# Multiplying the last quarter of each expert's down weights as plain float32 instead of splitting it

## The chip, the cores and the metric

The kernel runs on one core of one Trainium2 chip. The metric is the device time of one execution in microseconds (us). A core has five engines that run side by side, each through its own list of instructions in order: TensorE (PE, with its weight loads shown as PEld), VectorE (DVE), ScalarE (ACT), GpSimd (POOL) and SyncE (SP), which here starts most DMA transfers. They wait for each other through semaphores.

## The reference

One layer of a decoder for 2048 tokens of width 1024: a mixer (projection, matrix memory, a recurrence, output projection), a router, and a mixture of 32 experts. Each token goes to two experts. Only the experts matter for the change:

```
gates = gates / jnp.sum(gates, axis=-1, keepdims=True)
...
def expert_block(args):
    xb, e = args
    hid = jax.nn.silu(xb @ w_gate[e]) * (xb @ w_up[e])
    return hid @ w_down[e]
```

Tokens are sorted by expert and cut into blocks of up to 128. `w_gate[e]` and `w_up[e]` are 1024 x 512, `w_down[e]` is 512 x 1024, all float32. The result of a block is scaled by the gates and added to each token's row; a layer norm ends the layer.

## The kernel before

The products are made to float32 accuracy from pieces: a float32 operand w is split into a rounded part `wh` in the type float32r, which TensorE multiplies in one pass, and the remainder `wl = w - wh`, and a product x·w is the three products xh·wh + xl·wh + xh·wl. For weights, ACT makes `wh` (`copy`, L1313) and DVE makes `wl` (`sub`, L1316).

The experts are the last phase, `moe_phase`. The 32 experts are taken in a fixed order. Each has 12 raw tiles of 128 x 1024 (512 KB each): four of gate, four of up, four of down (a "quarter" of down is 128 rows of the 512). `load` starts their transfers on SP's queue into 9 buffers with the tag raw (`RAW = 39 - 2 * SPL`, SPL = 15). `high` makes the `wh` of a tile, `low` its `wl` and then starts the load of the tile nine further on, since the subtraction was the last reader of the raw tile. `wh` and `wl` have 15 buffers each, so all 12 of an expert and the first three of the next (`AHEAD = 3`) are split at a time. Raw tiles, `wh` and `wl` together fill 39 tiles.

`block` computes up to 128 tokens: 24 matmuls of 512 columns for gate, Silu on ACT, 48 matmuls of 256 columns for up in two halves, the products with Silu(gate) on DVE (L1445, tile th), four transposes of the hidden values through PE, the split of these into `hh` (ACT) and `hl` (DVE), then `down(k)` for the four quarters, six matmuls each:

```
for a, b in ((hh, dh), (hh, dl), (hl, dh)):
    for n in range(2):
        mm(pd[n], a[:, ks], b[:, n * CH:(n + 1) * CH], ...
```

The order on each engine is the order in which the code is written (`keep`). In the first block of an expert the splits stand between PE's steps: tiles 3 to 8 ahead of the gate's matmuls, `high` of 9 to 11 behind Silu, `low` of the down tiles between the steps of up and down, the last of them (`low(e, 11)`) together with the transposed rows of the next expert (`xh`, `xl`), and at the end the three tiles of the next expert. Then ACT scales the two halves of the result into yo (L1515), POOL multiplies yo by a row (`scaled`, L1597) and starts the scattered addition to memory (L1601), both behind the branch on the expert's token count (L1718).

An expert with more than 128 tokens takes that branch: a rest of at most 64 tokens goes to `narrow` (under the branch L1684), which packs the rounded part and the remainder of 64 tokens side by side in 128 columns, so that four matmuls make a quarter of down instead of six; a larger rest takes `block` again. Only the first block of an expert loads and splits.

Of the kernel before, what the change touches and what calls it, by code (L numbers as in the profile page):

```python
# [7 lines left out]
F32 = mybir.dt.float32  # L8
F32R = mybir.dt.float32r
# [6 lines left out]
P = 128  # L16
D = 1024
# [3 lines left out]
CH = 512  # L21
# [5 lines left out]
NE = 32  # L27
DFF = 512
# [1260 lines left out]
def moe_phase(tc, A, cn, u2_dram, lists, z_dram, mods_dram, out, nstat=4):  # L1289
    nc = tc.nc  # L1290
    ident, cnt = cn["ident"], cn["cnt"]
    SPL, LATE = 15, 9
    RAW, AHEAD = 39 - 2 * SPL, SPL - 12
    NZ = 6

    order = [4 * (i % 8) + i // 8 for i in range(NE)]
# [1 line left out]
    with ExitStack() as es:  # L1298
# [7 lines left out]
        def mm(*a, **k):  # L1306
            keep(nc.tensor.matmul(*a, **k))  # L1307
# [4 lines left out]
        def copy(o, i, scale=1.0):  # L1312
            keep(nc.scalar.activation(o, i, AF.Copy, scale=scale))  # L1313

        def sub(o, a, b):
            keep(nc.vector.tensor_sub(o, a, b))  # L1316


        raws = {}
        ws = {}  # L1320
        nload = [0]

        def load(upto, queue=nc.sync):
            while nload[0] < min(upto, 12 * NE):
                e, i = divmod(nload[0], 12)
                e = order[e]
                t = wp.tile([P, D], F32, tag="raw", name="raw", bufs=RAW)
                if i < 8:
                    k = i % 4
                    src = A["w_up" if i >= 4 else "w_gate"][0, e, 256 * k:256 * (k + 1), :]  # L1330
                    op = queue.dma_start(t.rearrange("p (k f) -> p k f", f=DFF), src.rearrange("(k p) f -> p k f", p=P))
                else:
                    op = queue.dma_start(t, A["w_down"][0, e, P * (i - 8):P * (i - 7), :])
                if queue is nc.gpsimd:
                    keep(op)
                raws[nload[0]] = t
                nload[0] += 1

        def high(e, *ks):
            if e < NE:  # L1340
                for i in (12 * e + k for k in ks if 12 * e + k not in ws):
                    h = wp.tile([P, D], F32R, tag="wh", name="wh", bufs=SPL)
                    copy(h, raws[i])
                    ws[i] = [h]

        def low(e, *ks):
            if e < NE:
                for i in (12 * e + k for k in ks if len(ws[12 * e + k]) == 1):
                    lo = wp.tile([P, D], F32R, tag="wl", name="wl", bufs=SPL)
                    sub(lo, raws.pop(i), ws[i][0].bitcast(F32))  # L1350
                    ws[i].append(lo)
                    load(i + 1 + RAW)

        g2row = tp.tile([P, D], F32, name="g2row")
        nc.scalar.dma_start(g2row, mods_dram[3:4].to_broadcast([P, D]))
# [72 lines left out]
        def block(e, f, nxt=None, first=False, ahead=lambda: None):  # L1428
# [18 lines left out]
            def hid_t(q):  # L1447
                for k in range(qs[q].start, qs[q].stop, P):
                    tpose(pth[:, k:k + P], th[:, k:k + P])
                copy(hh[:, qs[q]], pth[:, qs[q]])  # L1450
                sub(hl[:, qs[q]], pth[:, qs[q]], hh[:, qs[q]].bitcast(F32))

            def down(k):
                dh, dl = ws[12 * e + 8 + k]
                ks = slice(k * P, (k + 1) * P)
                for a, b in ((hh, dh), (hh, dl), (hl, dh)):
                    for n in range(2):
                        mm(pd[n], a[:, ks], b[:, n * CH:(n + 1) * CH], start=(k == 0 and b is dh and a is hh),
                           stop=(k == 3 and a is hl))

            th = tp.tile([P, DFF], F32, tag="th", name="th")
            hh = tp.tile([P, DFF], F32R, tag="hh", name="hh")
            hl = tp.tile([P, DFF], F32R, tag="hl", name="hl")
            if first:
                high(e, *range(AHEAD, 9))
                low(e, *range(AHEAD, 8))
# [4 lines left out]
                    ffn(pg, 0, slice(0, DFF), n, ks)  # L1471
            keep(nc.scalar.activation(th, pg, AF.Silu))
            if first:
                high(e, 9, 10, 11)
                low(e, *range(8, LATE))
            for q, n in ((0, 0), (0, 1), (1, 0), (0, 2)):
                ffn(pu[q], 4, qs[q], n)
# [18 lines left out]
                step(1)  # L1496
                out(0)
            if first:
                low(e, *range(LATE + 2, 12))
                high(e + 1, 0)  # L1500
            if nxt:
                out(1)
# [17 lines left out]
        def narrow(e, f):  # L1520
# [9 lines left out]
            def split(o, pt):  # L1530
                copy(o[:, :, lo], pt)
                sub(o[:, :, hi], pt, o[:, :, lo].bitcast(F32))
# [20 lines left out]
                keep(nc.vector.tensor_add(o, pp[lo], w))  # L1553

            th = tp.tile([P, DFF], F32, tag="th", name="th")[lo]
            h2 = tp.tile([P, 4, P], F32R, tag="hh", name="h2")
            cs = slice(0, DFF // 2), slice(DFF // 2, DFF)
            pd = [ps.tile([P, CH], F32, tag="pd", name="pd", bufs=2) for _ in range(2)]

            def hid_t(q):  # L1560
                pt = ps.tile([P, CH], F32, tag="tr", name="tr", bufs=3)
                for k in range(2):
                    c = (2 * q + k) * P
                    tpose(pt[:, k * H:(k + 1) * H], th[:, c:c + P], ident[lo, lo])
                split(h2[:, 2 * q:2 * q + 2, :], pt[:, 0:P].rearrange("p (k t) -> p k t", t=H))

            def down(k):
                for b in range(2):
                    for n in range(2):
                        mm(pd[n], h2[:, k, :], ws[12 * e + 8 + k][b][:, n * CH:(n + 1) * CH],  # L1570
                           start=(k + b == 0), stop=(k + b == 4))

            for q, c in enumerate(cs):
                pg = ps.tile([P, CH], F32, tag="gui", name="pg", bufs=1)
# [7 lines left out]
            down(0)  # L1582
            hid_t(1)
            down(1)
            down(2)
            down(3)
            yo = tp.tile([P, D], F32, tag="yoi", name="yo")[lo]
            for n in range(2):
                ns = slice(n * CH, (n + 1) * CH)
# [268 lines left out]
```

## Time and profile before

| | |
|---|---|
| median of 3 runs | 2823.99 us (2820.49 to 2826.87) |
| profiled execution | 2821.55 us, of which the span from first to last instruction is 2819.7 us |
| mean granted clock of TensorE | 0.977 |
| PE busy | 2598.6 us (92%) |
| DVE busy | 2026.8 us (72%) |
| ACT busy | 1316.7 us (47%) |
| POOL busy | 751.0 us (27%) |
| expert phase | about 1846 to 2820 us of the span |

Busy time is the sum of the durations of an engine's instructions. A duration of a matmul overlaps the next one's start, since they are pipelined; what one costs PE is the distance of its start from the next start. A wait is idle time of an engine in front of an instruction, put down to what released it.

### The profile page before, as it was taken

What the parts mean: (1) busy time and instruction counts of PE and PEld (TensorE: products, weight loads), DVE (VectorE), ACT (ScalarE), POOL (GpSimd) and SP (SyncE); (2) the same over time, 40 slices, a digit from 0 to 9 for tenths busy, and PEclk for the clock granted to TensorE, in tenths of its full rate; (3) what the DMA queues carried; (4) which work ended last, traced back from release to release, by engine and by line L of the source; (5) the groups of instructions that cost most, each with busy time, mean ns of one, the idle gap of its engine ahead of it and who ended that gap; (6) DMA issues with size and microseconds to landing.
All of it is one profiled execution on the core that took longest, in us unless ns stands there. A gap on an engine that the chain in (4) does not pass through costs nothing. (4 is left out here: it accounts for less than half of the span.)

```text
span 2819.7 us, 39064 instructions
## 1 busy us (share of the span) xinstructions
PE 2598.6 (92%) x13528; PEld 2153.5 (76%) x13528; DVE 2026.8 (72%) x3908; ACT 1316.7 (47%) x1871; POOL 751.0 (27%) x593
## 2 busy tenths in 40 slices
PE   5999999999999999999989999769999999999991
PEld 3688887888778888888868888558887787777871
DVE  7967788887796677667766667665668756776857
ACT  4734434444572444444521111055556655665746
POOL 2212222322122222222221221222323323232323
PEclk9999999999999999999999999879999999999996
DMA  8223444322222222222263333377778878897976
GB/s 248 62 69 83 127 120 129 105 81 67 90 77 82 61 68 79 79 65 67 82 225 102 105 105 112 120 250 264 240 229 310 302 227 304 280 366 244 336 253 254
DMA packets 301858, 456.15 MB, mean 162 GB/s; under 512 B 21296, under 2 KB 169240, under 8 KB 301536
## 3 DMA queue, kind: packets, MB, share of 16 engines
q1 hardware_dynamic: 285040, 396.20, 41.8%
q0 software_dynamic: 16064, 54.57, 7.5%
q8 instruction: 144, 2.36, 0.3%
q10 hardware_dynamic: 432, 1.57, 0.2%
q14 instruction: 178, 1.46, 0.2%
HBM read 386.03 MB, written 66.24 MB: 160 GB/s over the span
## 5 line engine op out<-in xcount | busy, mean ns | idle before, releaser
L97 PE MATMUL acc<-ul,wh 128*128 128x512 f32 x1536 | 621.6, 405 | 0.6 <-ACT xx L445 0.6
L97 PE MATMUL acc<-uh,wl 128*128 128x512 f32 x1536 | 603.2, 393 | 0.0
L97 PE MATMUL acc<-uh,wh 128*128 128x512 f32 x1536 | 602.0, 392 | 0.0
L1316 DVE TENSOR_TENSOR wl<-raw,wh 128x1024 fp32r<-128x1024 f32 x384 | 479.1, 1292 | 37.8 <-ACT wh L1313 32.8
L1313 ACT ACTIVATE wh<-raw 128x1024 fp32r<-128x1024 f32 x384 | 383.0, 1053 | 85.9 <-PEq L1692 19.6
L97 PEld LDWEIGHTS acc<-uh,wl 128*128 128x128 f32 x1536 | 289.7, 189 | 62.9
L97 PEld LDWEIGHTS acc<-ul,wh 128*128 128x128 f32 x1536 | 290.5, 189 | 56.2 <-ACT xx L445 0.7
L97 PEld LDWEIGHTS acc<-uh,wh 128*128 128x128 f32 x1536 | 290.7, 189 | 55.3 <-issue 0.7
L953 PE MATMUL po<-wol,yh 128*128 128x512 f32 x512 | 201.9, 394 | 0.6 <-DVE wol L971 0.4
L953 PE MATMUL po<-woh,yh 128*128 128x512 f32 x512 | 201.5, 394 | 0.0
L1307 PE MATMUL pgu<-wh,xl 128*128 128x256 f32 (+1 forms) x936 | 180.2, 323 | 13.3 <-PEq L1718 6.1
L1307 PE MATMUL pgu<-wl,xh 128*128 128x256 f32 (+1 forms) x936 | 184.7, 327 | 7.1 <-DVE wl L1316 7.1
L1307 PE MATMUL pgu<-wh,xh 128*128 128x256 f32 (+1 forms) x936 | 179.3, 325 | 9.5 <-ACT wh L1313 5.9
L1597 POOL TENSOR_TENSOR yo<-yo,g2row 128x1024 f32<-128x1024 f32 (+1 forms) x39 | 107.5, 2756 | 247.1 <-issue 151.4
L322 ACT ACTIVATE wh<-raw 128x1024 fp32r<-128x1024 f32 x96 | 101.4, 1056 | 146.3 <-PE acc L97 135.5
L953 PE MATMUL po<-woh,yl 128*128 128x512 f32 x512 | 163.4, 400 | 5.9 <-ACT woh L970 5.9
L1307 PEld LDWEIGHTS pgu<-wh,xh 128*128 128x128 f32 x936 | 142.0, 190 | 32.3 <-ACT wh L1313 10.0
L1307 PEld LDWEIGHTS pgu<-wh,xl 128*128 128x128 f32 x936 | 136.0, 189 | 38.7 <-issue 26.2
L1307 PEld LDWEIGHTS pgu<-wl,xh 128*128 128x128 f32 x936 | 137.1, 188 | 31.4 <-DVE wl L1316 19.5
L986 ACT ACTIVATE yh<-yr 128x1024 fp32r<-128x1024 f32 x31 | 32.9, 1061 | 253.2 <-PE po L953 239.0
L1388 POOL DMA_INDIRECT xg<-u_dram,rows x49 | 56.8, 1160 | 263.7 <-PE tr L1310 249.8
L323 DVE TENSOR_TENSOR wl<-raw,wh 128x1024 fp32r<-128x1024 f32 x92 | 117.7, 1280 | 8.7 <-ACT wh L322 7.5
(417 smaller groups left out, 5058.9 us busy)
## 6 DMA issues: line engine op xcount, KB each, us to landing
raw<-in_w_gate_dram SPq DMA_DIRECT2D x128, 512.0 KB
raw<-in_w_up_dram SPq DMA_DIRECT2D x128, 512.0 KB
raw<-in_w_down_dram SPq DMA_DIRECT2D x128, 512.0 KB
raw<-in_w_in_dram SPq DMA_DIRECT2D x96, 512.0 KB
x<-in_w_ada_dram SPq DMA_DIRECT2D x32, 512.0 KB
y_dram<-y SPq DMA_DIRECT2D x64, 256.0 KB
yr<-y_dram SPq DMA_DIRECT2D x31, 512.0 KB
x<-in_x_dram SPq DMA_DIRECT2D x27, 512.0 KB
```

The lines of the kernel that those rows point to most:

```text
L97: tc.keep_in_program_order(nc.tensor.matmul(*a, **k))
L322: keep(nc.scalar.activation(wh, raw, AF.Copy))
L323: keep(eng.tensor_sub(wl, raw, wh.bitcast(F32)))
L953: tc.keep_in_program_order(nc.tensor.matmul(*a, **k))
L986: nc.scalar.activation(h, raw, AF.Copy)
L1307: keep(nc.tensor.matmul(*a, **k))
L1313: keep(nc.scalar.activation(o, i, AF.Copy, scale=scale))
L1316: keep(nc.vector.tensor_sub(o, a, b))
L1388: keep(nc.gpsimd.indirect_dma_start(out=xg, out_offset=None, in_=src, in_offset=bass.IndirectOffsetOnAxis(ap=row, axis=0)))
L1597: keep(nc.gpsimd.tensor_mul(yo, yo, g2row[0:yo.shape[0]]))
```

## The change

The constants become SPL = 14, RAW = 9, AHEAD = 3: 28 buffers for 14 split tiles, 9 raw ones, and two buffers of a new tag wn, 39 tiles as before. Only 11 tiles of an expert are now loaded into raw buffers and split. The fourth quarter of down goes, unsplit, into a wn tile; its load stands in `load` in front of the fourth gate tile's. In `block` the fourth quarter of the transposed hidden values is copied as plain float32 into `hn` by ACT, `hh` and `hl` are 384 columns wide instead of 512 (so the second pair of copy and subtraction covers 128 columns instead of 256), and `down(3)` is two plain float32 matmuls. `high` of tile 11 and `low` of tile 11 are gone. In `narrow` the float32 pair stands between `down(1)` and `down(2)`, with 64 columns of hidden values.

```diff
-    SPL, LATE = 15, 9
-    RAW, AHEAD = 39 - 2 * SPL, SPL - 12
+    SPL, LATE = 14, 9
+    RAW, AHEAD = 37 - 2 * SPL, SPL - 11
...
-            while nload[0] < min(upto, 12 * NE):
-                e, i = divmod(nload[0], 12)
-                e = order[e]
+            while nload[0] < min(upto, 11 * NE):
+                n, i = divmod(nload[0], 11)
+                e = order[n]
+                if i == 3:
+                    w = wp.tile([P, D], F32, tag="wn", name="wn", bufs=2)
+                    queue.dma_start(w, A["w_down"][0, e, 3 * P:4 * P, :])
+                    ws[12 * n + 11] = [w]
...
-                    load(i + 1 + RAW)
+                    load(11 * e + i % 12 + 1 + RAW)
...
-                copy(hh[:, qs[q]], pth[:, qs[q]])
-                sub(hl[:, qs[q]], pth[:, qs[q]], hh[:, qs[q]].bitcast(F32))
+                c = slice(qs[q].start, min(qs[q].stop, 3 * P))
+                copy(hh[:, c], pth[:, c])
+                sub(hl[:, c], pth[:, c], hh[:, c].bitcast(F32))
+                if q:
+                    copy(hn, pth[:, 3 * P:4 * P])
...
             def down(k):
+                if k == 3:
+                    for n in range(2):
+                        mm(pd[n], hn, ws[12 * e + 11][0][:, n * CH:(n + 1) * CH], start=False, stop=True)
+                    return
...
-                high(e, 9, 10, 11)
+                high(e, 9, 10)
...
-                low(e, *range(LATE + 2, 12))
...
-                split(h2[:, 2 * q:2 * q + 2, :], pt[:, 0:P].rearrange("p (k t) -> p k t", t=H))
+                pt = pt[:, 0:P].rearrange("p (k t) -> p k t", t=H)
+                if q:
+                    copy(hn, pt[:, 1, :])
+                    pt = pt[:, 0:1, :]
+                split(h2[:, 2 * q:min(2 * q + 2, 3), :], pt)
...
             down(1)
+            for n in range(2):
+                mm(pd[n][lo], hn, ws[12 * e + 11][0][:, n * CH:(n + 1) * CH], start=False, stop=False)
             down(2)
-            down(3)
```

PE, the last three quarters of down in the first block of an expert and the first gate matmuls of the next (pd is the result, pgu the gate or up sum), before:

```order
L1307 MATMUL pd<-wh,hh 128x512 x2
L1307 MATMUL pd<-wl,hh 128x512 x2
L1307 MATMUL pd<-wh,hl 128x512 x2
L1307 MATMUL pd<-wh,hh 128x512 x2
L1307 MATMUL pd<-wl,hh 128x512 x2
L1307 MATMUL pd<-wh,hl 128x512 x2
L1307 MATMUL pd<-wh,hh 128x512 x2
L1307 MATMUL pd<-wl,hh 128x512 x2
L1307 MATMUL pd<-wh,hl 128x512 x2
L1708 TENSOR_LOAD cnt
L1307 MATMUL pgu<-wh,xh 128x512 x4
```

and now:

```order
L1307 MATMUL pd<-wh,hh 128x512 x2
L1307 MATMUL pd<-wl,hh 128x512 x2
L1307 MATMUL pd<-wh,hl 128x512 x2
L1307 MATMUL pd<-wh,hh 128x512 x2
L1307 MATMUL pd<-wl,hh 128x512 x2
L1307 MATMUL pd<-wh,hl 128x512 x2
L1307 MATMUL pd<-wn,hn 128x512 x2
L1725 TENSOR_LOAD cnt
L1307 MATMUL pgu<-wh,xh 128x512 x4
L1307 MATMUL pgu<-wh,xl 128x512
```

The last six matmuls of the block have become two that read the unsplit tile.

DVE, one first block from its start to the branch (subtractions of weights into wl, of hidden values into hl, of the next expert's rows into xl), before:

```order
L1316 TENSOR_TENSOR wl<-raw,wh 128x1024 x6
L1445 TENSOR_TENSOR th<-th,pgu 128x256
L1316 TENSOR_TENSOR wl<-raw,wh 128x1024
L1316 TENSOR_TENSOR hl<-tr,hh 128x256
L1445 TENSOR_TENSOR th<-th,pgu 128x256
L1316 TENSOR_TENSOR wl<-raw,wh 128x1024
L1316 TENSOR_TENSOR hl<-tr,hh 128x256
L1316 TENSOR_TENSOR xl<-tr,xh 128x512
L1316 TENSOR_TENSOR wl<-raw,wh 128x1024
L1316 TENSOR_TENSOR xl<-tr,xh 128x512
L1316 TENSOR_TENSOR wl<-raw,wh 128x1024 x3
L1718 COMPARE_AND_BRANCH
```

and now:

```order
L1316 TENSOR_TENSOR wl<-raw,wh 128x1024 x6
L1450 TENSOR_TENSOR th<-th,pgu 128x256
L1316 TENSOR_TENSOR wl<-raw,wh 128x1024
L1316 TENSOR_TENSOR hl<-tr,hh 128x256
L1450 TENSOR_TENSOR th<-th,pgu 128x256
L1316 TENSOR_TENSOR wl<-raw,wh 128x1024
L1316 TENSOR_TENSOR hl<-tr,hh 128x128
L1316 TENSOR_TENSOR xl<-tr,xh 128x512 x2
L1316 TENSOR_TENSOR wl<-raw,wh 128x1024 x3
L1735 COMPARE_AND_BRANCH
```

The subtraction between the two of xl is gone, and the second of hl covers half the columns.

SP, the loads of one expert's block around the start of it, before:

```order
L1333 DMA raw<-in_w_down_dram 128x1024 x2
L1709 REGISTER_ALU
L1854 BRANCH_PREFETCH_HINT
L1331 DMA raw<-in_w_gate_dram 128x2x512 x4
L1331 DMA raw<-in_w_up_dram 128x2x512 x4
L1333 DMA raw<-in_w_down_dram 128x1024 x2
```

and now:

```order
L1338 DMA raw<-in_w_down_dram 128x1024
L1336 DMA raw<-in_w_gate_dram 128x2x512
L1726 REGISTER_ALU
L1871 BRANCH_PREFETCH_HINT
L1330 DMA wn<-in_w_down_dram 128x1024
L1336 DMA raw<-in_w_gate_dram 128x2x512 x3
L1336 DMA raw<-in_w_up_dram 128x2x512 x4
L1338 DMA raw<-in_w_down_dram 128x1024 x2
```

The first gate tile of the next expert is loaded ahead of the block's start, one tile earlier in the queue than before, and the wn tile follows it.

## Rows read from the trace of the kernel before

**Rows 1.** Stretches: from:to, us, busy of PE, PEld, DVE, ACT, POOL; clock, DMA share, GB/s.

```profile
2100.00:2200.00 100.00, 91.86 (x541) 76.30 (x540) 70.25 (x85) 61.75 (x91) 32.30 (x17) 1.00 0.86 301
2400.00:2500.00 100.00, 92.87 (x528) 77.34 (x526) 81.33 (x83) 70.61 (x87) 26.89 (x13) 1.00 0.92 315
```

**Rows 2.** Waits of PE, 1820 to 2820: total us, times, longest us.

```profile
PE pg L1307 <- DVE x L1316: 11.1, 8, 2.3
PE tr L1310 <- DVEq L1684: 7.8, 3, 4.6
PE pgu L1307 <- DVE wl L1316: 7.1, 25, 1.0
PE pgu L1307 <- PEq L1718: 6.1, 20, 0.4
PE pgu L1307 <- ACT wh L1313: 5.9, 11, 2.0
PE pd L1307 <- ACT hh L1313: 5.0, 4, 1.5
```

**Rows 3.** Groups of PE's matmuls in down: count, then busy us, mean ns.

```profile
L1307 PE MATMUL pd<-wh,hh 128*128 128x512 f32 x312 | 103.9, 414 | 5.0 <-ACT hh L1313 5.0
L1307 PE MATMUL pd<-wh,h 128*128 128x512 f32 x64 | 20.9, 407 | 0.0
```

**Rows 4.** Plain float32 matmuls: line L97 by operation (ns), and timeline (start, us).

```profile
L97 PE MATMUL acc<-xc,wab x16: 590/592/697, 89.2 to 128.5; 128*128 128x512 f32 x16
...
89.15 1.88 PE L97 MATMUL acc<-xc,wab 128*128 128x512 f32 x4
90.87 0.27 PE L100 MATMUL tr<-ident,gB 128*128 128x128 f32 x1
```

**Rows 5.** Timeline of PE: fourth quarter of down, then the next block's start.

```profile
2307.65 0.63 PE L1307 MATMUL pd<-wh,hh 128*128 128x512 f32 x2
...
2309.05 1.09 PE L1307 MATMUL pgu<-wh,xh 128*128 128x512 f32 x4
```

**Rows 6.** Timeline of all engines around that block's end, in order of start.

```profile
2306.33 0.60 ACT L1313 ACTIVATE xh<-tr 128x512 fp32r<-128x512 f32 x1
...
2307.27 0.69 DVE L1316 TENSOR_TENSOR xl<-tr,xh 128x512 fp32r<-128x512 f32 x1
...
2307.87 3.49 DVE L1316 TENSOR_TENSOR wl<-raw,wh 128x1024 fp32r<-128x1024 f32 x3
...
2309.07 1.27 ACT L1313 ACTIVATE yo<-pd,l 128x512 f32<-128x512 f32 x2 [0.24 <-issue]
...
2310.56 3.08 POOL L1597 TENSOR_TENSOR yo<-yo,g2row 128x1024 f32<-128x1024 f32 x1 [4.28 <-issue]
...
2312.27 8.13 DVE L1316 TENSOR_TENSOR wl<-raw,wh 128x1024 fp32r<-128x1024 f32 x6 [0.90 <-ACT wh L1313]
```

**Rows 7.** Timeline of PE and PEld in the same block's up, to the first transpose.

```profile
2317.25 1.11 PE L1307 MATMUL pgu<-wh,xh 128*128 128x256 f32 x8
...
2318.20 0.87 PE L1307 MATMUL pgu<-wl,xh 128*128 128x256 f32 x6
...
2319.31 0.51 PE L1307 MATMUL pgu<-wl,xh 128*128 128x256 f32 x2 [0.24 <-DVE wl L1316]
...
2320.78 0.20 PEld L1310 LDWEIGHTS tr<-ident,th 128*128 128x128 f32 x2 [0.22 <-DVE th L1445]
```

**Rows 8.** Timeline of POOL at a block with a rest.

```profile
2371.41 2.41 POOL L1597 TENSOR_TENSOR yo<-yo,g2row 128x1024 f32<-128x1024 f32 x1 [4.95 <-issue]
```

**Rows 9.** Timeline at two narrow blocks: PE's start of one, ACT ahead of another.

```profile
2014.20 0.39 PE L1307 MATMUL pg<-wh,x 128*128 128x256 f32 x1 [0.72 <-DVE x L1316]
...
2179.80 1.06 ACT L1313 ACTIVATE wh<-raw 128x1024 fp32r<-128x1024 f32 x1 [1.22 <-DMA raw<-in_w_gate_dram]
```

**Rows 10.** Timeline of ACT in an expert without a rest that follows such experts.

```profile
2436.42 1.06 ACT L1313 ACTIVATE wh<-raw 128x1024 fp32r<-128x1024 f32 x1 [2.25 <-DMA raw<-in_w_down_dram]
```

**Rows 11.** Waits of SP, 1820 to 2820: its own branch instruction.

```profile
SPq L1718 <- SPq L1718: 10.3, 15, 5.2
```

More of the change, by code (lines that the diff above doesn't have):

```diff
@@ L1335, in load @@
                     keep(op)
-                raws[nload[0]] = t
+                raws[12 * n + i] = t
                 nload[0] += 1
@@ L1457, in down @@
                     for n in range(2):
-                        mm(pd[n], a[:, ks], b[:, n * CH:(n + 1) * CH], start=(k == 0 and b is dh and a is hh),
-                           stop=(k == 3 and a is hl))
+                        mm(pd[n], a[:, ks], b[:, n * CH:(n + 1) * CH], start=(k == 0 and b is dh and a is hh), stop=False)
             th = tp.tile([P, DFF], F32, tag="th", name="th")
-            hh = tp.tile([P, DFF], F32R, tag="hh", name="hh")
-            hl = tp.tile([P, DFF], F32R, tag="hl", name="hl")
+            hh = tp.tile([P, 3 * P], F32R, tag="hh", name="hh")
+            hl = tp.tile([P, 3 * P], F32R, tag="hl", name="hl")
+            hn = tp.tile([P, P], F32, tag="hn", name="hn")
             if first:
@@ L1555, in narrow @@
             th = tp.tile([P, DFF], F32, tag="th", name="th")[lo]
-            h2 = tp.tile([P, 4, P], F32R, tag="hh", name="h2")
+            h2 = tp.tile([P, 3, P], F32R, tag="hh", name="h2")
+            hn = tp.tile([P, P], F32, tag="hn", name="hn")[:, lo]
             cs = slice(0, DFF // 2), slice(DFF // 2, DFF)
@@ L1570, in down @@
                         mm(pd[n], h2[:, k, :], ws[12 * e + 8 + k][b][:, n * CH:(n + 1) * CH],
-                           start=(k + b == 0), stop=(k + b == 4))
+                           start=(k + b == 0), stop=(k + b == 3))
             for q, c in enumerate(cs):
```

## Prediction

> **What bounds the kernel now.** First the busy shares by stretch. In two stretches of 100 us of the expert phase PE is busy 91.9 and 92.9 us, DVE 70 and 81, and the transfers use 0.86 and 0.92 of their engines [rows 1]. So PE sets the pace there, and each microsecond added to its list is added to the time unless PE gets it back from its own waits. These are the second view [rows 2]: the six kinds shown sum to 43 us. Only they can pay for more PE work: a subtraction or a copy less on DVE or ACT is worth nothing in itself. Third the timeline of single blocks, to see what each wait hangs on. Outside the expert phase the instructions stay as they are.
>
> **Price on PE.** In the trace a quarter of down in a full block lasts from 2307.65 to the next block's first matmul at 2309.05, 1.40 us for six matmuls [rows 5]. Before, plain float32 matmuls of the same 128 x 512 shape stand at one place: the four records from 89.15 to the next instruction at 90.87 take 1.72 us, 0.43 a record [rows 4]. The kernel's code there has eight such matmuls and the trace sixteen records, so one matmul is two records, 0.86 us, and the new pair costs 1.72 us. That is 0.32 us more than the six. Their number: 312 matmuls wh·hh at 8 a block make 39 full blocks; 64 in narrow at 8 make 8 narrow blocks [rows 3]. Full: 39 x 0.31 (1.72 - 1.41, the mean over several quarters) = 12.1. Narrow: four matmuls at 1.40/6 each are 0.94, so 8 x 0.78 = 6.3. Together **+18.4 us**, all on the path. The hidden values have 64 columns in narrow, but PE's time goes by the 512 columns that stream, so I take the same price for it; the least it could be is that of the old four matmuls, which would take 6.3 away.
>
> In the Trainium skill, "Perfetto Trace Analysis", section "Engine Utilization", halves the output rate for FP32_LOW_HIGH, which by an estimate from its 307.2 G elements/s is 0.43 us for such a matmul and 0.85 for the pair. "FP8 and Floating Point Precision", section "TensorE Precision Notes", says that true float32 is four passes, twice as long. By the first the sum's first term would be about -22, by the second +18.4. The trace agrees with the second: 1.72 for two.
>
> **What the splitting chain gives back.** Twenty first blocks directly follow an expert without a rest (the 20 waits at the branch L1718, [rows 2], 0.3 us each, stay). Such a block takes 19.62 us. About 15 of them show one pattern. The block's last matmul has ended at about 2309.05. DVE ends its three subtractions for the next expert only at 2307.87 + 3.49 = 2311.36. ACT scales the result by 2310.34. POOL's multiplication is issued at 2310.56 and lasts 3.08, against 2.41 at 2371.41 [rows 6, 8]: the 0.67 is what remained of DVE's subtractions. DVE's first subtraction behind the branch starts at 2312.27 and must wait for POOL in turn: six subtractions take 8.13 where they would take about 7.0 (three take 3.49). So the eighth gate/up tile is late. Six matmuls of up from 2318.20, spaced as the eight before them (0.95/8 = 0.119), would be over at 2318.91, but the next starts at 2319.31 [rows 7]: 0.40 lost. The product on DVE behind it is late as well, 0.22 at the transpose's weight load [rows 7]; from starts of matmuls I read 0.18 there, 0.58 in all; I take 0.54 since two or three of the blocks show less.
>
> After: the subtraction of tile 11 (1.2 us) between DVE's two xl is gone and hl is half as long. But the second xl waits for ACT's xh, which ended at 2306.93, while xl started only at 2307.27 [rows 6]. So the three last subtractions end earlier by 0.2 to 0.3 at most, not by 1.4. ACT has no copy of tile 11 (1.05 us, earlier in the block) and a new copy into hn of about 0.3. The block's end meanwhile moves 0.31 later. Against the end DVE is thus about 0.54 ahead: POOL then waits 0.1 to 0.3 instead of 0.67, releases DVE some 0.4 to 0.5 earlier, and the waits of 0.40 and 0.18 close. The block's period becomes 19.62 + 0.31 - 0.54 = 19.4. **15 x -0.54 = -8.1 us.** Three first blocks have a full rest behind them (the DVEq L1684 waits, 3 times, [rows 2]); there PE hangs on DVE's last subtractions in the same way: 3 x -0.54 = **-1.6**.
>
> **What the transfers give back.** Nine raw buffers now hold 9 of 11 tiles instead of 9 of 12, and the float32 quarter has its own two. On SP's queue the first gate tile of the next expert goes ahead of the block and wn behind it, so gate and up tiles are asked for about one load earlier and the last down tiles about two. At the 301 to 315 GB/s of these stretches [rows 1] a load of 0.524 MB is 1.7 us, in the busiest moments less. The bytes stay the same.
>
> Narrow blocks wait for their rows on DVE, 11.1 us in 8 waits [rows 2]. The least one is 0.72 [rows 9], the chain transposes, ACT, DVE itself; 8 x 0.72 = 5.8 stays. The remaining 5.3 is ACT: it waits in order for the next expert's third gate tile (1.22 us at 2179.80, [rows 9]) ahead of the narrow block's copies. A load one place earlier covers 1.2 to 1.7 us, so I take nearly all of it: **-5.1**; bounds 0 and -5.3.
>
> Several experts without a rest in a row are short of data: ACT waits 2.25 for a down tile at 2436.42 [rows 10], and down waits for ACT's hh queued behind that copy, 5.0 us in 4 waits [rows 2]. The tile that was waited for last is now fetched early as wn or is two loads earlier; but a row of such experts needs 12 loads in 19.6 us, more than the 315 GB/s of the stretch brings, so a lead is used up: half, **-2.5**; bounds 0 and -5.0. The wn load waits on SP for PE's last use of the buffer, the down of the expert before the one then running; that is met when SP passes the branch, and behind it only gate tiles queue.
>
> **Sum:** +18.4 - 8.1 - 1.6 - 5.1 - 2.5 = **+1.1 us**. Against the profiled execution (2821.55, span 2819.7) that is 2822.7; the median of the runs is 2.4 higher, so **2825 us**. One more thing moves it: SP's branch instruction took up to 5.2 us at times [rows 11], and as the code is shifted in memory these stalls may fall elsewhere: 3 us either way.
>
> **Rivals.**
>
> *Slower: the chain POOL, DVE, PE moves along with the block's end.* The place is the end of a first block. If ACT delivers the three next tiles no earlier (it has the hn copy between hh and xh, and xh in front of the first of the three), DVE ends its third subtraction 0.31 later too, and POOL still waits. The point is whether DVE ends at least 0.3 earlier against the last matmul. For it speaks that ACT's xh and not DVE already held the second xl to within 0.34 us. Price: 8.1 and 1.6 don't come back, +9.7: 2825 + 9.7 = 2834.7. The Trainium skill ("SBUF — State Buffer", section "Who interferes with whom") says that DVE and POOL take the shared port for a whole instruction, whoever starts first. By that, POOL's multiplication still holds DVE up when it comes just ahead of it, so part of the wait stays; the 3.08 and the 8.13 agree. If the transfers don't help either, only +18.4 is left: 2842.
>
> *Faster: the loads were what mattered.* With two more loads in flight all waits for transfers go: the other 2.5 at hh, and the 5.9 us of waits for wh [rows 2], 8.4 us together, and of the 7.8 in front of full rests [rows 2] what is not in the sum, 6.2. That gives 2825 - 8.4 = 2816.6 without and 2810 with the last. For it speaks that the DMA share is below 1 in both stretches [rows 1]; against it that the largest wait before a full rest is a single one of 4.6 us early in the phase, and that 5.9 in 11 waits has several causes.
>
> *The pair is cheap:* each new float32 matmul takes one record of 0.43 us. Then 39 x (0.86 - 1.41) = -21.5 and 8 x (0.86 - 0.94) = -0.6, with the returns of 17.3 largely void since PE would be no later: about 2798. Sixteen records for eight matmuls [rows 4] speak against it. It is what the halved rate of the Trainium skill ("Perfetto Trace Analysis", "Engine Utilization") would give.
>
> **How the numbers follow.** The forecast, returns about equal to the price, has 0.48: 2825, from 2818 to 2830. Slower by the chain 0.30 (2833 to 2842), faster by the loads 0.18 (2810 to 2817), the cheap pair 0.03, the rest shared by unknown stalls. The range of 2811 to 2838 leaves out the cheap pair, the upper third of the slower case and the edge of the faster one, about 0.15 to 0.2. A measurement of this kernel can tell about 0.2%, 5.6 us, from no change; so faster 0.20, same 0.49, slower 0.31.
>
> **What the profile after would show.** Right: pd<-wn,hn with four records a block, 1.72 us from its first start to the next block's start; single blocks at 19.4 us; POOL's multiplication below 2.8 in them; no wait of 0.40 in up; PE's wait for x near 6 us in 8 times; the wait for hh about halved. Wrong: a period of 19.9 with the 0.40 still there (the chain moved along); a pair other than 1.72 (the whole first term goes by 39); more waits of SP at the wn load with gate tiles late behind it.

## The result and the profile after

The changed kernel takes 2841.85 us in the median of 7 runs (2833.4 to 2844.3), against 2824.72 for the kernel before on the same chips; the ratio is 1.0054 with an interval of 1.0042 to 1.0066. By the ratio it is slower by about 15 us (17 between the two medians), outside the range that was given. The profiled execution took 2842.94 us, its span is 2841.2 us, 21.5 us longer than that of before.

The engines' sums on the page of the changed kernel: PE has 24.5 us more than before (2598.6), DVE 45 less, ACT 30 less.

```profile
span 2841.2 us, 38907 instructions
...
PE 2623.1 (92%) x13450; PEld 2141.9 (75%) x13450; DVE 1981.4 (70%) x3876; ACT 1286.9 (45%) x1886; POOL 755.0 (27%) x593
```

The waits of PE in the expert phase of the changed kernel (total us, times, longest us), to be laid beside [rows 2]:

```profile
PE pgu L1307 <- PEq L1735: 17.7, 20, 4.3
...
PE pgu L1307 <- ACT wh L1313: 6.8, 8, 2.3
...
PE pgu L1307 <- DVE wl L1316: 5.9, 22, 0.4
...
PE pg L1307 <- DVE x L1316: 5.4, 8, 0.7
...
PE tr L1310 <- DVEq L1701: 3.6, 3, 1.3
...
PE pd L1307 <- ACT hh L1313: 0.5, 1, 0.5
```

Three lines fell: the narrow blocks' wait for x from 11.1 to 5.4, the wait for hh from 5.0 to 0.5, the wait in front of full rests (L1684 before, L1701 now) from 7.8 to 3.6. The wait for wl, from which the forecast took most, fell only from 7.1 to 5.9, and still occurs 22 times, where it had occurred 25 times. One line grew: at the branch behind an expert without a rest (L1718 before, L1735 now) PE waits 17.7 instead of 6.1, up to 4.3 at once, where the longest had been 0.4.

ACT's waits for the transfers of weight tiles, from the phase's first block on, before:

```profile
ACT wh L1313 <- DMA raw<-in_w_gate_dram: 15.8, 15, 2.9
ACT wh L1313 <- DMA raw<-in_w_down_dram: 12.5, 15, 2.3
ACT wh L1313 <- DMA raw<-in_w_up_dram: 2.3, 6, 0.7
```

and now:

```profile
ACT wh L1313 <- DMA raw<-in_w_gate_dram: 1.3, 2, 0.9
```

They are all but gone, 1.3 us instead of 30.6.

Now the end of one first block of the changed kernel, on all engines, to be laid beside [rows 5 to 7]:

```profile
2337.97 0.28 ACT L1313 ACTIVATE hh<-tr 128x128 fp32r<-128x128 f32 x1 [2.55 <-PE tr L1310]
...
2338.61 0.28 ACT L1313 ACTIVATE hn<-tr 128x128 f32<-128x128 f32 x1 [0.36 <-DVE hl L1316]
...
2338.78 0.59 ACT L1313 ACTIVATE xh<-tr 128x512 fp32r<-128x512 f32 x1
...
2340.21 0.60 ACT L1313 ACTIVATE xh<-tr 128x512 fp32r<-128x512 f32 x1
...
2341.00 1.88 PE L1307 MATMUL pd<-wn,hn 128*128 128x512 f32 x4
...
2341.45 3.49 DVE L1316 TENSOR_TENSOR wl<-raw,wh 128x1024 fp32r<-128x1024 f32 x3
...
2344.08 3.12 POOL L1614 TENSOR_TENSOR yo<-yo,g2row 128x1024 f32<-128x1024 f32 x1 [4.44 <-issue]
...
2345.85 8.12 DVE L1316 TENSOR_TENSOR wl<-raw,wh 128x1024 fp32r<-128x1024 f32 x6 [0.92 <-ACT wh L1313]
...
2352.89 0.50 PE L1307 MATMUL pgu<-wl,xh 128*128 128x256 f32 x2 [0.26 <-DVE wl L1316]
```

The pair is four records, 0.43 apart, as the four of [rows 4]. The next block's first matmul is recorded with 0.80 from 2342.32, but the one behind it starts at 2342.95; at their spacing of 0.23 the next block runs on from 2342.72, 1.72 us after the pair's start. But the new copy hn waits 0.36 for DVE's hl, and ACT's xh behind it comes 0.81 after the start of hh, where it came 0.29 after in the kernel before (2304.62 to 2304.91 there). So DVE's three last subtractions are hardly earlier against the block's end, POOL's multiplication still lasts 3.12, DVE's six subtractions still 8.12, and PE still waits in up. Such a block has a period of 19.85 us instead of 19.62.

And one of the blocks in which PE was late at the branch, with the granted clock behind it (stretch, us, busy of PE, PEld, DVE, ACT, POOL, clock, DMA share, GB/s):

```profile
2243.72 0.40 PE L1307 MATMUL pgu<-wh,xl 128*128 128x512 f32 x1
2248.41 1.62 PE L1307 MATMUL pgu<-wh,xl 128*128 128x512 f32 x3 [4.30 <-PEq L1735]
...
2248.00:2253.00 5.00, 4.59 (x11) 3.65 (x12) 3.67 (x4) 4.76 (x6) 2.57 (x3) 0.50 1.00 342
```

PE goes without work for 4.3 us, and behind that the granted clock is at the lower of its two levels (0.50, 1.2 GHz) for some 5 us. Of 25.37 us this block lost 5.5. Counted from 0, with rests as blocks of their own, blocks 12, 15, 20, 30, 31 and 40 lost in such ways: their lengths are 23.12, 22.79, 25.37, 23.16, 25.59 and 22.20 where the others have 19.85, together 23.1 us. In block 12 it is not PE but ACT that comes out of the branch late, and PE waits for its wh:

```profile
2088.76 2.95 ACT L1313 ACTIVATE wh<-raw 128x1024 fp32r<-128x1024 f32 x3 [3.85 <-ACTq L1725]
...
2089.86 1.22 PE L1307 MATMUL pgu<-wh,xh 128*128 128x512 f32 x2 [2.14 <-ACT wh L1313]
```

The last narrow block lost 2.9 us more (17.05 from its first matmul to the end of its last, where the other seven have 14.18 to 14.20), but not at a branch: DVE stopped for 1.23 us between two of its instructions without a wait, PE waited for it, and the pair behind ran at a lower clock.

```profile
2756.80 0.42 DVE L1597 TENSOR_TENSOR th<-th,part 64x256 f32<-64x256 f32 x1 [1.23 <-issue]
...
2757.36 0.30 PE L1310 MATMUL tr<-ident,th 64*128 64x64 f32 x2 [1.73 <-DVE th L1597]
...
2758.73 3.61 PE L1307 MATMUL pd<-wn,hn 128*64 128x512 f32 x4
```

The kernel before has a loss that looks like one of these and is another: the wait of 4.6 in front of the full rest behind its block 2 [rows 2]. There ACT waits for the transfer of a gate tile, DVE for ACT and PE for DVE. Before:

```profile
1895.85 1.06 ACT L1313 ACTIVATE wh<-raw 128x1024 fp32r<-128x1024 f32 x1 [2.94 <-DMA raw<-in_w_gate_dram]
...
1896.93 1.23 DVE L1316 TENSOR_TENSOR wl<-raw,wh 128x1024 fp32r<-128x1024 f32 x1 [1.99 <-ACT wh L1313]
...
1898.48 1.94 PE L1310 MATMUL tr<-ident,xg 128*128 128x128 f32 x8 [4.55 <-DVEq L1684]
```

and now:

```profile
1893.58 1.06 ACT L1313 ACTIVATE wh<-raw 128x1024 fp32r<-128x1024 f32 x1 [0.91 <-DMA raw<-in_w_gate_dram]
...
1896.21 1.06 PE L1310 MATMUL tr<-ident,xg 128*128 128x128 f32 x8 [1.26 <-DVEq L1701]
```

From the start of block 2 to the next first block it took 44.84 us before and takes 39.86 now. I take that for a gain of the earlier loads; e1_raw8 below bears it out.

I call a branch late on an engine if the time from its branch instruction to its first instruction behind it is over 0.8 us above the usual one. Of the 20 branches behind an expert without a rest, the kernel before had one late on DVE and one on SP; the changed kernel has four late on PE, three on ACT, two on DVE, one on SP.

**Theories.** (1) The chain: hn on ACT put off xh by as much as the removed work had gained, so the waits of the chain stayed. (2) The late branches: either the place of the code in memory decides (layout), or the earlier loads get in the way of the code's own fetch (traffic), or they are chance.

### The profile page after: what moved, and what is told of

It is laid out like the page before. It is cut to its first block, busy times and chain, and to the rows that moved or that the text cites. A ratio compares the mean times of both kernels' runs of the same rounds, so it can differ in the third digit from the quotient of the medians.

```text
span 2841.2 us, 38907 instructions
## 1 busy us (share of the span) xinstructions
PE 2623.1 (92%) x13450; PEld 2141.9 (75%) x13450; DVE 1981.4 (70%) x3876; ACT 1286.9 (45%) x1886; POOL 755.0 (27%) x593
## 5 line engine op out<-in xcount | busy, mean ns | idle before, releaser
L97 PE MATMUL acc<-ul,wh 128*128 128x512 f32 x1536 | 621.5, 405 | 0.6 <-ACT xx L445 0.6
L97 PE MATMUL acc<-uh,wl 128*128 128x512 f32 x1536 | 603.3, 393 | 0.0
L97 PE MATMUL acc<-uh,wh 128*128 128x512 f32 x1536 | 601.8, 392 | 0.0
L1316 DVE TENSOR_TENSOR wl<-raw,wh 128x1024 fp32r<-128x1024 f32 x352 | 432.9, 1280 | 49.3 <-ACT wh L1313 44.9
L1313 ACT ACTIVATE wh<-raw 128x1024 fp32r<-128x1024 f32 x352 | 348.2, 1051 | 75.5 <-ACTq L1725 20.6
L97 PEld LDWEIGHTS acc<-uh,wl 128*128 128x128 f32 x1536 | 289.6, 189 | 62.8
L97 PEld LDWEIGHTS acc<-ul,wh 128*128 128x128 f32 x1536 | 290.5, 189 | 56.2 <-ACT xx L445 0.7
L97 PEld LDWEIGHTS acc<-uh,wh 128*128 128x128 f32 x1536 | 290.7, 189 | 55.3 <-issue 0.7
L1307 PE MATMUL pgu<-wh,xl 128*128 128x256 f32 (+1 forms) x936 | 184.3, 328 | 24.4 <-PEq L1735 17.7
L1307 PE MATMUL pgu<-wh,xh 128*128 128x256 f32 (+1 forms) x936 | 192.2, 340 | 10.7 <-ACT wh L1313 6.8
L1614 POOL TENSOR_TENSOR yo<-yo,g2row 128x1024 f32<-128x1024 f32 (+1 forms) x39 | 114.8, 2944 | 247.9 <-issue 139.8
L1307 PEld LDWEIGHTS pgu<-wh,xh 128*128 128x128 f32 x936 | 143.5, 192 | 45.4 <-issue 14.8
L322 ACT ACTIVATE wh<-raw 128x1024 fp32r<-128x1024 f32 x96 | 101.3, 1056 | 146.7 <-PE acc L97 136.1
L323 DVE TENSOR_TENSOR wl<-raw,wh 128x1024 fp32r<-128x1024 f32 x92 | 117.4, 1276 | 7.1 <-ACT wh L322 5.9
```

What stands on the lines that cost most here:

```text
L97: tc.keep_in_program_order(nc.tensor.matmul(*a, **k))
L322: keep(nc.scalar.activation(wh, raw, AF.Copy))
L323: keep(eng.tensor_sub(wl, raw, wh.bitcast(F32)))
L1614: keep(nc.gpsimd.tensor_mul(yo, yo, g2row[0:yo.shape[0]]))
```

## The experiments

All compare with the kernel before on the same chip. Counts of late branches are those of the profiled execution.

### Where the late branches come from

**e1_same**, the changed kernel once more.

> The changed kernel unchanged, for a second profile and as the measure of this group. In its first profile PE, ACT or DVE came out of the branch behind an expert without a rest 2 to 4.5 us late in six of 20 cases, where before had one, a late DVE. If the place of an instruction in memory decides (layout), the same experts (the 12th, 15th, 20th, 30th, 31st and 40th block) are late again. If it is chance or traffic, others are late, and the time moves between 2833 and 2844 with their number.

2840.94 us (ratio 1.0058). The PE branches of blocks 15, 20 and 31 were late again, and so were the same three on ACT, two on DVE and one on SP, at the same experts; only the fourth of PE was not, by little (0.75 us above the usual time). It isn't chance. The blocks' lengths agree with the first profile within 0.4 us, but for the last narrow one.

**e1_pad**, all code of the expert phase moved by 64 instructions on three engines:

```diff
+        for _ in range(64):
+            pt = ps.tile([P, CH], F32, tag="tr", name="tr", bufs=3)
+            tpose(pt[:, 0:P], ident)
+        ...
         load(RAW)
```

> The changed kernel with 64 more instructions each on PE (transposes nobody reads), ACT and DVE ahead of the expert phase, which move all code behind them in memory; they run while PE waits for the first rows and cost 0 to 10 us there. Layout: the late branches fall on other experts or vanish, at another total (0 to 17 us less in the phase). Traffic: the same number as in the unmoved kernel, 4 to 6, 16 to 20 us of them.

2860.18 us. One branch late on PE, four on ACT, five on DVE, one on SP, all of them at other experts than on the same engine before: layout. They are eleven where the unmoved kernel had ten. Of the 19 us more than in e1_same some 7 are not theirs: the first block of the phase starts at 1860.0 us, where it started at 1853.4. Blocks with none late stayed at 19.85.

**e1_raw8**, one raw buffer less (the buffers of the layer norm at the end follow it):

```diff
-    RAW, AHEAD = 37 - 2 * SPL, SPL - 11
+    RAW, AHEAD = 36 - 2 * SPL, SPL - 11
```

> The changed kernel with 8 raw buffers instead of 9, so that every load except wn starts one tile later. If late branches come from code being fetched beside weight transfers that now run into the branch (traffic), they become fewer, about as before (0 to 2). If from layout, their number and places stay. The waits of narrow blocks for x should rise again from 5.4 to some 8 to 11 us and those of down for hh from 0.5 to some 3 to 5.

2846.6 us. The late branches were those of the changed kernel, at the same experts on the same engines (4, 3, 2 and 1), though all transfers ran later: PE's 4.30 in block 20 was 4.27. Traffic falls, as far as a shift of one tile can tell. The waits for x rose to 8.1, as expected; that for hh did not return. Block 2 with its rest is back at 44.53 us, with ACT waiting twice for gate tiles (1.59 and 1.58): its loss in the kernel before was one of transfers.

**e2_before_pad**, the kernel before with the 64 instructions.

> The kernel before with the same 64 more instructions each on PE, ACT and DVE ahead of the expert phase; nothing else changed. If late branches are a matter of where code lies, and the kernel before merely had few of them (one DVE and one SP), this one has more, between 3 and 8, and is 5 to 20 us slower beyond the 6 us that the added instructions cost in the first experiment of this kind. If they belong to the change itself (its loads, its shorter PE code), it has one or two as before and is within 8 us of it.

2823.74 us, ratio 1.0010 (0.9997 to 1.0022): no slower. In its profile ACT is late three times and SP once, DVE no more. So the places move in this kernel too, but I expected more loss than came. The three late ACT do cost some 9 us (blocks of 20.91, 24.02 and 23.07 instead of 19.62), and block 2 with its rest gives 5.7 back (39.13 us instead of 44.84), since ACT's wait for the gate tile falls from 2.94 to 1.00. Here the phase begins 7.5 us later, which may have given the loads their lead; that was not tested. So the equal total doesn't show that late branches cost this kernel nothing.

### The chain

**e1_hn_dve**, the copy made by the other engine:

```diff
-                    copy(hn, pth[:, 3 * P:4 * P])
+                    keep(nc.vector.tensor_copy(hn, pth[:, 3 * P:4 * P]))
```

> The changed kernel with the copy hn made by DVE instead of ACT, behind hl. If the 0.5 us by which the hn copy and its wait for hl put off ACT's xh are why the chain POOL, DVE, PE gave nothing back, a block of an expert without a rest falls from 19.85 to 19.4 or 19.5 us, POOL's multiplication from 3.1 to about 2.7, and the wait of 0.42 in up goes; about 7 us less in all, late branches apart. If ACT's order is not the cause, the blocks stay at 19.85.

2828.97 us, ratio 1.0027 (1.0010 to 1.0045), 12 us less than e1_same. Blocks without a late branch have 19.21 us, less than the forecast's 19.4. The timeline of one:

```profile
2350.69 0.59 ACT L1313 ACTIVATE xh<-tr 128x512 fp32r<-128x512 f32 x1
...
2351.04 0.28 DVE L1459 COPY hn<-tr 128x128 f32<-128x128 f32 x1
...
2352.12 0.60 ACT L1313 ACTIVATE xh<-tr 128x512 fp32r<-128x512 f32 x1
...
2353.55 1.88 PE L1307 MATMUL pd<-wn,hn 128*128 128x512 f32 x4
...
2356.38 2.73 POOL L1614 TENSOR_TENSOR yo<-yo,g2row 128x1024 f32<-128x1024 f32 x1 [4.19 <-issue]
...
2364.23 1.11 PE L1307 MATMUL pgu<-wl,xh 128*128 128x256 f32 x8
```

xh starts 0.17 after hh does, the second xh 1.43 before PE's pair, where it was 0.79 before it in the changed kernel. POOL's multiplication falls to 2.73, and up's eight matmuls run without a stop. The copy of 0.28 on DVE lies in a gap, on ACT it did not. Theory (1) stands. The late branches fell elsewhere (two on PE, one on DVE) but for SP's, so the 12 us are not the chain's alone.

**e3_hn_first**, the copy on ACT, in front of DVE's hl:

```diff
-                sub(hl[:, c], pth[:, c], hh[:, c].bitcast(F32))
                 if q:
                     copy(hn, pth[:, 3 * P:4 * P])
+                sub(hl[:, c], pth[:, c], hh[:, c].bitcast(F32))
```

> The changed kernel with ACT's hn copy in front of DVE's hl subtraction instead of behind it. Of the 0.52 us by which ACT's xh came later, 0.36 are the wait for DVE and the rest the copy itself less what the narrower hh saves. If the wait is what kept the chain from closing, blocks of experts without a rest fall from 19.85 to 19.5 or 19.6; if the copy alone does, they stay above 19.75. Late branches as in the changed kernel, since the code has the same length.

Blocks of 19.37 us, better than either guess, with POOL at 2.91; 2838.43 us in all, as two branches on PE, three on ACT, two on DVE and one on SP were late: DVE's and SP's and one of ACT's at the changed kernel's places, the others elsewhere, although no code was added or taken away. So the place of the code isn't all that decides. As for the chain: of the 0.64 between 19.85 and 19.21 the wait of hn for hl was 0.48 and the copy's own place on ACT 0.16.

**e2_pair**, the price by itself: the kernel before with two float32 matmuls of the rounded parts for the last quarter of full blocks; the remainders of that quarter are left out of the product.

```diff
+                if k == 3:
+                    for n in range(2):
+                        mm(pd[n], hh[:, ks].bitcast(F32), dh[:, n * CH:(n + 1) * CH].bitcast(F32), ...)
+                    return
```

> The kernel before with all its splitting, its loads and its 15 buffers, and only the fourth quarter of down in full blocks made by two plain float32 matmuls of the rounded parts (the remainders of that quarter are left out of the product; narrow blocks unchanged). It measures the price by itself. Price of 1.72 for 1.40 and nothing given back: a block of an expert without a rest 19.62 + 0.31 = 19.9 us or a little less, since DVE's chain has 0.31 more to itself (19.6 if that closes the wait of 0.40 fully); full blocks of a rest 17.12 + 0.31 = 17.4. If the pair cost only 0.86, blocks of a rest would be 16.6.

2822.82 us, ratio 1.0008 (0.9995 to 1.0022): the price of the pair in 39 full blocks cannot be seen in the total. In a block of an expert without a rest:

```profile
2348.19 1.88 PE L1307 MATMUL pd<-wh,hh 128*128 128x512 f32 x4
...
2349.50 1.50 PE L1307 MATMUL pgu<-wh,xh 128*128 128x512 f32 x4
...
2351.02 3.15 POOL L1601 TENSOR_TENSOR yo<-yo,g2row 128x1024 f32<-128x1024 f32 x1 [4.19 <-issue]
...
2352.80 8.13 DVE L1316 TENSOR_TENSOR wl<-raw,wh 128x1024 fp32r<-128x1024 f32 x6 [0.91 <-ACT wh L1313]
...
2358.88 1.47 PE L1307 MATMUL pgu<-wl,xh 128*128 128x256 f32 x8
```

The pair costs PE 1.72 here too, yet the period stays 19.62. PE's stop in up shrinks from 0.40 to 0.26 and the rest is taken up elsewhere in the loop; POOL still takes 3.15. PE does not set the pace of these blocks, the loop through ACT, DVE and POOL does. In blocks of a full rest, which load and split nothing, the price is there: from the first gate matmul to the end of the last of down, five of the seven take 17.59 to 17.77 us in the kernel before and 17.90 to 18.07 here, 0.29 to 0.34 more each (the other two are lengthened in the kernel before by other stops).

### Can the late branches be had out of the way

**e2_late_hint**: each engine gets a hint that lets it fetch the code of the likely side of a branch. It is given at a block's start, as soon as the count is read; here, with hn on DVE, at the start of down, from a copy of the count that DVE makes there.

```diff
+                late = sp.tile([1, 1], cnt.dtype, tag="late", name="late", bufs=2)
+                keep(nc.vector.tensor_copy(late, cnt[0:1, e:e + 1]))
+                ns.append(nc.values_load(late[0:1, 0:1], min_val=0, max_val=S))
+                tc.mark_branch_hint_location(f"more{i}", hint=ns[0] > P, ...)
```

> The changed kernel with hn made by DVE, and with each engine's branch prefetch hint moved from the start of a block to the start of its down (the count is read there through a small copy by DVE, which costs DVE about 0.4 us in a gap). If a late branch is one whose target was fetched at the hint and lost since, as the engine's own code ran on, nearly all late branches vanish (0 or 1 instead of 4) and the time falls by 8 to 15 us against the same kernel with the early hint (2829). If what matters is only the place of the target, or if 5 us are too short for the fetch, there are as many or more.

2901.77 us. The hint stands 3.8 us ahead of PE's branch now. PE is later at 13 of the 20 branches, by 0.9 to 3.5 us, and on time at seven (2.7 us from the branch to going on, as with the early hint); its waits there are 35.5 us. DVE is late twice. The readings of the count cost besides, 31 stops of PE of up to 0.7, and PE waits 39.4 us for gathered rows (xg), 22 more than with the early hint. **e2_before_late** does the same to the kernel before.

> The kernel before with the late hint alone. It had one late DVE and one late SP in its profile. If the late hint cures, these go and the time is 0 to 6 us less; if DVE's extra copy and the reading of the count put off the chain at the block's end, 31 blocks by 0.1 to 0.4 each, 3 to 12 us more.

2869.83 us, blocks of 20.29, PE late once and DVE twice. The edit costs 0.67 a block by itself, and the waits for gathered rows rise from 17.4 to 47.5 us. So neither run can say whether the early hint's code is lost; they show only that this late hint is no remedy.

**e3_no_hint**, the changed kernel without that hint.

```diff
-ahead=lambda: tc.mark_branch_hint_location(f"more{i}", hint=n > P, ...)
+ahead=lambda: None
```

> The changed kernel without the branch prefetch hint for the branch behind the first block. If a late branch is code that has to be fetched when the branch is taken, all 20 become late on PE, ACT and DVE, 2 to 4 us each, and 40 to 80 us are added. If lateness has to do with something else (semaphores, the count), the time stays at 2835 to 2845.

2859.74 us, some 19 us more, but only PE is late at all 20; ACT and SP never, DVE once, by 0.81. The branch instruction of the sequencers (count, shortest, median and longest in ns, first and last start), changed kernel:

```profile
L1735 PEldq COMPARE_BRANCH  x31: 77/371/6224, 1872.9 to 2742.9; - x31
```

kernel before:

```profile
L1718 PEldq COMPARE_BRANCH  x31: 77/360/475, 1870.4 to 2723.5; - x31
```

without the hint:

```profile
L1735 PEldq COMPARE_BRANCH  x31: 70/3505/6632, 1869.7 to 2757.9; - x31
```

Of the 31, 20 are taken. Without a hint these take 3.4 to 6.6 us, with it 0.36 to 0.48 in both kernels, but for the four late ones of the changed kernel, which take 3.8 to 6.2 as if the hint had not served them. On ACT and DVE my expectation failed: they don't need it.

The traces also hold the fetches of code, as packets of the DMA queues named instruction. Block 15 of the changed kernel, PE behind its late branch, and the one packet of q8 in the stretch from 2144 to 2145:

```profile
2147.42 1.35 PE L1307 MATMUL pgu<-wh,xl 128*128 128x512 f32 x3 [2.52 <-PEq L1735]
...
q8 instruction: 1, 0.02, 6.8%
```

In e3_no_hint each of PE's 20 branches has one such packet of 16384 bytes between the branch and PE's going on, which follows 1.4 to 1.7 us after the packet has ended. The four late branches of the changed kernel have the same, with 1.43 to 1.56 us; at the 16 on time no packet behind the branch ended more than 0.5 us before PE went on. In three of the four no packet of that queue came between hint and branch; in all 16 at least one did. So a late branch on PE is a wait for code, and in three cases of four the hint had brought none. The late branches of ACT, DVE and SP in the changed kernel have packets of 8192 bytes on q14 in their stops.

**e3_dve_pad24** and **e3_dve_pad48**, hn on DVE, with 24 and 48 added instructions.

> The changed kernel with hn made by DVE (2829 us, four late branches of some 17 us in its profile), and its code moved by 24 small instructions each on PE, ACT and DVE ahead of the expert phase. Layout: the late branches fall elsewhere, and blocks of experts without a rest stay at 19.21 where none is late; with one or two late ones the kernel is at 2812 to 2820 and beats the kernel before, with six it is at 2835.

> The same with 48 instructions each: a second draw of the layout, 2812 to 2838 by the number of late branches, with places other than those of the draw with 24.

2829.52 us (three late on PE, three on DVE, one on SP) and 2825.48 us (one on PE, two on ACT, two on DVE, one on SP). Blocks without a late branch have 19.21 in both. The totals differ by several us from draw to draw, and neither beats the kernel before (1.0025 and 1.0013; the second's interval, 0.9999 to 1.0026, takes in 1).

**e4_dve_hint_pe** (hn on DVE) and **e4_before_hint_pe** (the kernel before): the hint for PE, SP and POOL, not for ACT and DVE.

```diff
-engines=list(mybir.ALL_ENGINES)
+engines=[mybir.EngineType.PE, mybir.EngineType.SP, mybir.EngineType.Pool]
```

> The changed kernel with hn made by DVE, and the prefetch hint for the branch behind the first block given to PE, SP and POOL but not to ACT and DVE. If the hint makes ACT and DVE late (its target takes the place of code that is needed next), none of them is late here, PE is late at about two as in the same kernel with all hints, and the time is 2815 to 2824. If layout alone decides and the hint only helps, ACT and DVE are late as often or more, and the time is 2829 or above.

> The kernel before with the hint for that branch on PE, SP and POOL only. It had one late DVE there, none on ACT and PE. If the hint makes ACT and DVE late, the one goes and the time is 0 to 3 us less; if not, ACT and DVE are late at more branches and the time rises by 2 to 4 us for each.

2820.70 us, ratio 0.9992 (0.9980 to 1.0004), and 2821.34, ratio 0.9995 (0.9983 to 1.0008). Neither ACT nor DVE was late at any of the 20 branches in either (DVE once came 0.80 later than usual), PE three times and once, SP once in each. With hn on DVE that is 8 us less than with all hints, but PE was late twice and ACT and DVE together once there, so the 8 us can't be laid to ACT and DVE. It is the best form of the change, 20 us below the changed kernel, and level with the kernel before.

## Why the prediction was wrong, step by step

**The price of the pair on PE** was right in size in full blocks: 1.72 us for two float32 matmuls, four records, and 0.3 more in the full rests of e2_pair. The four passes of the Trainium skill ("FP8 and Floating Point Precision", "TensorE Precision Notes") agree with the trace here, 0.86 us a matmul against 0.23 for one of float32r, and the cheap pair is out. In narrow blocks the term was too small: undisturbed ones took 13.07 us from the first gate matmul to the end of the last of down and take 14.18, 1.11 more instead of 0.78, 2.6 us in eight. Wrong was "all on the path". In the 20 blocks behind an expert without a rest PE was not the pace: e2_pair gave it 0.31 more in each of them, and the period of the undisturbed ones stayed 19.62.

**"15 x -0.54 = -8.1 us" is the first step that failed.** The chain was the right one (POOL's multiplication, DVE's subtractions, the eighth tile, PE's stop), and so was the point named under the slower rival: whether DVE ends at least 0.3 earlier against the last matmul. It ended 0.09 earlier: 2344.94 against 2342.72, the pair's 1.72 after its start, is 2.22, before it was 2311.36 against 2309.05, 2.31. The working had a copy "of about 0.3" on ACT that cost nothing because ACT had lost one of 1.05. The copy of tile 11 had its place earlier in the block; the new one stood between hh and xh, on ACT's critical stretch, and waited 0.36 for DVE's hl. With the copy on DVE the period falls by 0.64. In the changed kernel the undisturbed blocks came out at +0.23 instead of -0.23, some 7 to 9 us over the blocks in question.

**The transfers** gave more than was forecast. ACT's waits for weight tiles fell from 30.6 us to 1.3, and with them the waits that the sum counts: x -5.7 (forecast -5.1), hh -4.5 (-2.5). Of the -4.2 at full rests 3.3 are the gate tile of block 2, which the prediction named only in its faster rival (the single wait of 4.6 us); in the other two PE's wait fell from 1.91 and 1.31 to 1.2, by 0.8 together where the -1.6 asked for 1.1. Three blocks of experts without a rest in a row, 20.96, 21.69 and 21.18 us long before, have 19.85 to 19.87 now. So what the faster rival said of the loads came true in part, and was hidden by the rest.

**"3 us either way" for stalls at branches is the second step that failed, and the larger one.** I had read it off SP alone [rows 11] and took the five microseconds to be hidden there. Not even that is sure: behind SP's late branch of the kernel before (at 2423.20) two loads of down tiles stood, and ACT waits 1.14 and 2.25 for down tiles in that block, which is 21.43 us long; two blocks with SP on time have like waits, so SP's share is not known. Late on PE, ACT or DVE the same stall is on the path and takes the clock down behind it. By late branches on PE, ACT and DVE the changed kernel lost 23.1 us in six blocks, the kernel before 1.15 in one (its block 40). With the 2.9 of the last narrow block, a stop of DVE that was not at a branch, the net is nearly 25 us, more than the 21.5 by which the span grew. What the change does apart from this is then some -3 us in the profiled executions, where the forecast had +1.1. That the two are near each other is luck: the chain gave 7 to 9 us too little and narrow blocks cost 2.6 too much, PE's price was not paid as such in 20 blocks, and the transfers made up for it. It is luck too that 2841.85 lies in the 2833 to 2842 of the slower rival: that one had the chain right, but no late branches, which made the time.

Shown: the late branches stay with a program over two profiles (e1_same) and with later loads (e1_raw8), and move when code is added ahead (e1_pad, e2_before_pad); on PE they are waits for a fetch of code. The Trainium skill has the mechanism in "Runtime: NRT & Kernel Launch", section "Instruction fetch mechanics": an engine holds a window of pages of its code, and a taken branch to a target outside it waits for a fetch. The trace agrees: at all 20 branches without a hint PE goes on 1.4 to 1.7 us after a packet of its code has ended. What stays open is why a hinted branch is late at one place and not at another: places moved even when two instructions changed places (e3_hn_first), and SP's late one moved in the padded kernels, though SP got none of the added instructions. Why some hints bring no code is not shown. Open is also whether the hint itself makes ACT and DVE late. Over the eleven profiles with the early hint on all engines each of them was late at 21 of 220 branches; without it (e3_no_hint and the two e4 kernels) ACT was late at none of 60 and DVE at one. That speaks for it, but no run shows how.

## What to carry to other kernels

Before a matmul is priced as on the path, ask for the period of the block: if PE has waits that close when PE gets slower, another loop sets it, and the small copy put on that loop costs more than the matmuls. Where the code has branches, expect several microseconds from any edit that moves code, and compare the blocks that no late branch disturbs before the totals. Before a stop at a branch is put down to its code, follow what each engine waited for: the largest one of the kernel before hung on a transfer. A copy that reads a tile which another engine is also reading may be made to wait for it: order the reader on the critical engine first, or give it to the engine with the gap.

## What the runs showed of the hardware

- A plain float32 matmul of 128 x 512 is two records of 0.43 us at the full clock, against 0.23 for one of float32r; at a granted clock of 0.50 a float32r matmul takes 0.43.
- PE's branch instruction, when taken, lasted 3.4 to 6.6 us without the hint and 0.36 to 0.48 with it where it was on time; PE itself stood idle for 48.3 us at the 20 branches without it. A packet of 16384 bytes of code ended 1.4 to 1.7 us before PE went on. In the late cases of the changed kernel ACT came 2.9 to 3.3 us later than usual, DVE 2.0 to 2.5.
- 4.3 us without work on PE were followed by a granted clock of 0.50 over some 5 us.
- Reading the count late, by an instruction of 0.28 to 0.31 us on each engine and a copy ahead of it, made the blocks of the kernel before 0.67 us longer; PE stopped at it 31 times for 14.8 us in all.
